# Order of loads, spills and operand making around the borders of the MLP's chunks, and the end of a chunk's MLP block by block

## The chip, the cores and the metric

The kernel runs on one core of a Trainium2 chip. The metric is device time in microseconds of one execution. TensorE (PE) does the matmuls; VectorE (DVE), ScalarE (ACT) and GpSimd (POOL) do everything elementwise; SyncE (SP) issues all DMA transfers of this kernel.

## What is computed

One layer of an encoder on two groups of tokens, 512 and 1024, which the kernel treats as three chunks of 512. The parts that matter here, from the reference:

```python
h = h + jnp.concatenate([o_attn, o_pool], axis=-1) @ w_out
m = _rmsnorm(h, norm_mlp_g)
h = h + jnp.square(jax.nn.relu(m @ w_up)) @ w_down
gate = jax.nn.sigmoid((_rmsnorm(h, norm_ple_g) @ w_ple_gate))
h = h + gate * (p_i @ w_ple_proj)
```

The model width is 1024, the MLP's inner width 4096, all numbers are float32. `_rmsnorm` divides each token by the root of its mean square.

## The kernel before

**Stages.** Input projection (to about 200 us), attention (to about 597), MLP (597 to 1685), gate and final norm (to the end). A float32 product is made from three matmuls: each operand is split in a high part (a cast on ACT) and a low part (a subtraction on DVE or POOL). All SBUF working tiles come from one pool of 49 slots of one size (`slot`); a tile is free when its last reader is done. Activations lie transposed, `hT[c][a]` being block a (of four) of chunk c, 128 x 1024.

**Attention's end.** A loop over `at` issues one group of scores per step, with the softmax and the weighing of earlier groups beside it, and takes pieces from `fill`, a list of other PE work. After it, `while fill` works off the eleven last pieces `po`, the output projection's last ones (twelve matmuls each); two chore steps follow each piece.

**MLP.** Three chunks c, each of 16 pairs g (`Pair`; a pair is two blocks of the inner width). A pair's up projection is seven products of 12 matmuls 128x256 in a scheme after Strassen, in the order 1, 6, 2, 5, 7, 3, 4 (`ORDER`), PSUM tiles px, py, pz, pq. Product i needs an operand tile pair `mo` (i of the chunk, made once) and a weight `w` (made for every pair from the raw weight `wur` by ACT and POOL in `feed`). Four `down` blocks (PSUM pd) of the previous pair go between the products, and each is added to `hT` by DVE (the line of h<-pd). 132 matmuls make a pair. Pairs are counted through, 0 to 47: chunk 1 begins with pair 16, chunk 2 with pair 32.

The MLP's input is never normalised. `h` itself is multiplied by w = the mean square plus epsilon, token by token (`raise_h`, one of four blocks after each product of pair 0), the squares of the up projection of plain h are added to it, and at the end of the chunk h is multiplied by the inverse of w (`invert`, `lower_h`). The DVE executes in the order written, so what stands behind a raise waits for w.

**Making the operands** (`make_m(c)`) is a generator of a chunk before its MLP: h is spilled to DRAM (`spill`, to `h_d`), two tiles m of it loaded per half b, squared on ACT (`sqm`, line 607) and summed; gains and differences are made; seven tiles `mm` per half are split high and low, and stored to `mo_d`; then the sum is split (`sh`), `wait(2)` passes two steps, and the w matmul with ones and one DVE step give w, stored to `w_d`. For chunk 0 each `mo` is loaded again right behind its stores (`load_mo(0, i)`); for the later chunks the loads follow the products of the previous chunk's last pair. `load_ms` brings w back at pair 0, behind the four `load_h`.

**End of a chunk.** During pair 1 of the next chunk `lower_h`, `stat_g` (squares of h summed on DVE, line 590, then the inverse root, spread over the partitions by matmuls), `store_h` (h to `hl_d`) and, for chunk 0, `put_in` (the gate's input split high on ACT, line 1114, low on DVE, line 1115, and stored to `hg_d`) are appended to `chores`.

**What sets the order.** PE, ACT, DVE and POOL execute in the order in which the program is written. Generators in the deque `chores` are advanced by `step()`, one step per product of the MLP (two per piece of the po tail), and only the front one moves. A `yield` therefore is a place where a product's work comes in between; `wait(n)` is n of them. SP's queue alone is ordered by the scheduler: it holds loads and stores, is worked through in order, and an entry waits until its tile is free or its data are there, with all behind it.

## Time and profile before

| | us |
|---|---|
| median of 3 runs (1873.69 to 1878.16) | 1873.84 |
| the profiled execution | 1874.47 |
| its span | 1872.7 |
| mean granted clock of TensorE | 0.983 |

The span is the time on the engines; 1.8 us of the execution lie around it. The profile's views that follow: the page's table of busy time by engine; waits (engine, tile and line that waited, and the engine or transfer whose work ended the wait); windows (the busy time of each engine between two times, with the granted clock as PEclk, and the share of DMA time); and rows of the timeline (start, duration, engine, line, operation, tile written <- tiles read, and in brackets the idle time before it and what ended it).

### The profile page before, as it was taken

How to read it: one execution, taken by the hardware profiler on the slowest of the kernel's cores; microseconds unless marked ns; L12 is line 12 of the kernel's file. 1: busy time of each engine (PE TensorE's matmuls, PEld its weight loads, DVE VectorE, ACT ScalarE, POOL GpSimd, SP SyncE). 2: the span in 40 equal slices, each digit the busy share in tenths (PEclk: the TensorE clock that was granted, in tenths of full speed). 3: DMA queues.
4: the chain of work that ended last, by engine and by line, in shares of the span. 5: the costliest groups of instructions: out<-in, count | busy, mean ns of one | idle time of the engine just before them, and what ended most of it. 6: DMA issues, size and time to landing. Idle time of an engine off the chain costs nothing.

```text
span 1872.7 us, 28563 instructions
## 1 busy us (share of the span) xinstructions
PE 1779.1 (95%) x10540; PEld 1551.8 (83%) x10540; DVE 1248.2 (67%) x1831; ACT 940.8 (50%) x1854; POOL 1030.5 (55%) x909
## 2 busy tenths in 40 slices
PE   9999899999969798999999998999999999999997
PEld 7888777988758687898888887898888898988887
DVE  5667856889864776665569676655686655566555
ACT  6344456678852555444545464445454445443332
POOL 3474864447642685755556475756566556652221
PEclk9999999999989899999999999999999999999998
DMA  6333553012373443532374533523642323362102
GB/s 240 113 136 130 186 208 134 29 68 102 142 247 117 159 147 136 180 113 91 109 284 145 188 133 138 197 90 124 270 164 91 112 91 103 100 242 79 57 10 82
DMA packets 83883, 256.84 MB, mean 137 GB/s; under 512 B 9888, under 2 KB 16416, under 8 KB 83744
## 3 DMA queue, kind: packets, MB, share of 16 engines
q1 hardware_dynamic: 83744, 255.02, 38.6%
q8 instruction: 83, 1.36, 0.3%
q14 instruction: 56, 0.46, 0.1%
HBM read 195.74 MB, written 59.24 MB: 136 GB/s over the span
## 4 chain that ended last, share of the span: by engine, by line
PE 47%; DVE 5%; ACT 3%; POOL 3%; issue 2%; DMA 2%; POOLq 0%; DVEq 0%; SPq 0%; ACTq 0%
PE pd L49 21%; PE pg L49 6%; PE px L49 5%; PE pz L49 5%; PE pq L49 5%; PE py L49 3%; PE pj L49 1%; POOL mm L634 1%; POOL w L784 1%; DVE h L834 1%; DVE r L883 1%; ACT w L783 1%; DMA w<-w_d 1%; DVE wd L814 1%; POOL wd L814 0%
## 5 line engine op out<-in xcount | busy, mean ns | idle before, releaser
L49 PE MATMUL pd<-r,wd 128*128 128x512 f32 x2304 | 576.7, 399 | 12.8 <-DVE r L883 12.2
L49 PEld LDWEIGHTS pd<-r,wd 128*128 128x128 f32 x2304 | 424.5, 190 | 105.4 <-DVE r L883 18.3
L784 POOL TENSOR_TENSOR w<-ws,w 128x512 fp32r<-128x512 f32 x192 | 272.8, 1424 | 242.7 <-ACT w L783 236.6
L784 POOL TENSOR_TENSOR w<-wur,w 128x512 fp32r<-128x512 f32 x144 | 211.4, 1479 | 167.0 <-ACT w L783 157.8
L834 DVE TENSOR_TENSOR h<-pd,h 128x1024 f32<-128x1024 f32 x192 | 233.8, 1218 | 91.7 <-PE pd L49 91.7
L783 ACT CAST w<-ws 128x512 fp32r<-128x512 f32 x192 | 118.5, 617 | 253.4 <-DVE ws L792 224.1
L461 POOL TENSOR_SCALAR pr<-pr,rr 128x512 f32<-128x512 f32 x160 | 111.1, 705 | 143.9 <-DVE rr L456 63.3
L814 DVE TENSOR_TENSOR wd<-wdr,wd 128x512 fp32r<-128x512 f32 x96 | 105.6, 1100 | 109.0 <-ACT wd L813 89.9
L49 PE MATMUL z<-w,x 128*128 128x512 f32 (+1 forms) x864 | 174.8, 358 | 1.9 <-ACT w L159 1.4
L49 PEld LDWEIGHTS pz<-mo,w 128*128 128x128 f32 x1152 | 151.7, 191 | 28.4 <-issue 20.3
L49 PE MATMUL pz<-mo,w 128*128 128x256 f32 x1152 | 154.9, 284 | 18.9 <-issue 14.2
L49 PEld LDWEIGHTS z<-w,x 128*128 128x128 f32 x864 | 142.6, 188 | 28.4 <-ACT w L159 3.3
L49 PE MATMUL pq<-mo,w 128*128 128x256 f32 x1152 | 156.8, 286 | 8.4 <-DVE c L867 4.8
L49 PEld LDWEIGHTS pq<-mo,w 128*128 128x128 f32 x1152 | 147.3, 194 | 9.6 <-issue 9.2
L49 PE MATMUL px<-mo,w 128*128 128x256 f32 x1152 | 153.1, 282 | 0.0
L49 PEld LDWEIGHTS px<-mo,w 128*128 128x128 f32 x1152 | 147.4, 190 | 4.0
L49 PE MATMUL pg<-hg,wg 128*128 128x512 f32 (+1 forms) x768 | 141.1, 338 | 0.2
L814 POOL TENSOR_TENSOR wd<-wdr,wd 128x512 fp32r<-128x512 f32 x96 | 129.1, 1345 | 10.8 <-ACT wd L813 10.8
L472 ACT CAST pt<-tp 128x512 fp32r<-128x512 f32 x160 | 88.3, 591 | 91.3 <-PE tp L53 84.0
L49 PEld LDWEIGHTS pg<-hg,wg 128*128 128x128 f32 x768 | 118.8, 188 | 17.8 <-DVE hg L1115 1.0
L473 DVE TENSOR_TENSOR pt<-tp,pt 128x512 fp32r<-128x512 f32 x160 | 104.2, 684 | 36.3 <-ACT pt L472 35.3
L813 ACT CAST wd<-wdr 128x512 fp32r<-128x512 f32 x192 | 118.8, 619 | 13.5 <-DMA wdr<-in_w_down_dram 11.5
(191 smaller groups left out, 2965.6 us busy)
## 6 DMA issues: line engine op xcount, KB each, us to landing
wur<-in_w_up_dram SPq DMA_DIRECT2D x96, 512.0 KB, 4.1
wdr<-in_w_down_dram SPq DMA_DIRECT2D x96, 512.0 KB, 4.3
mo_d<-mm SPq DMA_DIRECT2D x84, 256.0 KB, 2.6
mo<-mo_d SPq DMA_DIRECT2D x42, 512.0 KB, 6.3
h_d<-h SPq DMA_DIRECT2D x16, 512.0 KB, 2.9
h<-h_d SPq DMA_DIRECT2D x16, 512.0 KB, 8.4
xn<-in_xn_dram SPq DMA_DIRECT2D x12, 512.0 KB, 6.1
qs_d<-qs SPq DMA_DIRECT2D x12, 512.0 KB, 3.0
```

The lines of the kernel that those rows point to most:

```text
L49: last_pe[0] = nc.tensor.matmul(*a, **k).ins
L461: gp.tensor_scalar(p, p, rr, 1.0, op0=ALU.mult, op1=ALU.mult)
L472: sc.copy(self.pt[kt][:, 0], tp)
L473: ve.tensor_tensor(self.pt[kt][:, 1], tp, as32(self.pt[kt][:, 0]), op=ALU.subtract)
L634: el.tensor_tensor(out[:, 1], x, as32(out[:, 0]), op=ALU.subtract)
L783: sc.copy(t[:, 0], x)
L784: gp.tensor_tensor(t[:, 1], x, as32(t[:, 0]), op=ALU.subtract)
L813: sc.copy(hi, self.dr[i][:, h])
L814: (gp, ve)[i].tensor_tensor(lo, self.dr[i][:, h], as32(hi), op=ALU.subtract)
L834: ve.tensor_tensor(h, pd.rearrange("p (a b) -> p a b", a=2), h, op=ALU.add)
L883: ve.tensor_tensor(self.r[i][:, 1], x, as32(self.r[i][:, 0]), op=ALU.subtract)
```

## The change

`make_m` waits five steps, not one, behind the loads of m, and seven, not two, ahead of the w matmul. `load_mo(0, i)` leaves `make_m`: three are issued in the attention loop at steps 99 to 101, and four in the po tail. The first raw weights are loaded at step 96 instead of 94. The first pair's down weights and chunk 0's h are loaded ahead of the po tail and no longer at pair 0. `spill(2)` waits eight steps. For the chunks 0 and 1 `lower_h`, `stat_g`, `store_h` and `put_in` become one generator, `finishing`: a block is lowered on DVE; a step later stored and squared on ACT, and for chunk 0 the gate input's high part is made on ACT; a step later the square is added on POOL (128x1024, three of these and one of 128x512 a chunk, where DVE did it) and the gate input's low part is made on DVE and both are stored. Six steps pass after the sums, then the inverse root follows as before. The loads of h and w at the borders to chunk 1 and 2 stay where they are.

```diff
--- before.py
+++ after.py
@@ -612,7 +612,7 @@
             m = [slot([P, 2, CH], F32, f"m{c}_{2 * i + b}") for i in range(2)]
             for i in range(2):
                 load(m[i], h_d[c][2 * i + b])
-            yield
+            yield from wait(5)
             yield from lagged(squares_of(b, m))
             for i in range(2):
                 for h in range(2):
@@ -634,14 +634,12 @@
                         el.tensor_tensor(out[:, 1], x, as32(out[:, 0]), op=ALU.subtract)
                         for j in range(2):
                             sy.dma_start(mo_d[c][i][j][:, 2 * b:2 * b + 2], as32(out[:, j]))
-                        if c == 0 and b:
-                            load_mo(0, i)
                     yield (lambda x=x, out=out: sc.copy(out[:, 0], x)), low_part
             yield from lagged(pairs())
         sh = slot([P, 2, CH], F32R, f"sh{c}")
         sc.copy(sh[:, 0], acc[:, 0])
         el.tensor_tensor(sh[:, 1], acc[:, 0], as32(sh[:, 0]), op=ALU.subtract)
-        yield from wait(2)
+        yield from wait(7)
         bc = tp_ps(f"w{c}")
         for i in range(2):
             pe.matmul(bc, ones_sb, sh[:, i], start=i == 0, stop=i == 1)
@@ -679,7 +677,10 @@
         out = []
         yield from squares(c, "g", out, e)
         yield from wait((3, 2, 3)[c])
-        bc = yield from rsqrt_rows([out.pop()[:, 0]], CH, f"g{c}")
+        yield from spread_g(c, out.pop())
+
+    def spread_g(c, acc):
+        bc = yield from rsqrt_rows([acc[:, 0]], CH, f"g{c}")
         if c != 1:
             bcs["t"] = slot([P, 2, CH], F32, f"bcs{c}")
         sc.copy(bcs["t"][:, c % 2], bc)
@@ -701,6 +702,7 @@
     away = set()
 
     def spill(c):
+        yield from wait(8 if c == 2 else 0)
         for a in range(4):
             sy.dma_start(h_d[c][a], hT[c][a])
         away.add(c)
@@ -1001,8 +1003,10 @@
         if at == 82:
             for a in range(4):
                 load_h(2, a, h_d[2][a])
-        if at == 94:
+        if at == 96:
             pairs[0].load_up()
+        if at > 98 and at < 102:
+            load_mo(0, ORDER[at - 99])
         for un_ in done:
             un_.finish()
         joining = done
@@ -1060,9 +1064,14 @@
             act()
             yield
 
+    pairs[0].load_down()
+    for a in range(4):
+        load_h(0, a, h_d[0][a])
     while fill:
         fill.popleft()()
         step(2)
+        if len(fill) % 2 and len(fill) < 8:
+            load_mo(0, ORDER[6 - len(fill) // 2])
         if len(fill) % 2 == 0 and len(fill) < 8:
             next(feeding)
     ps_free()
@@ -1106,28 +1115,43 @@
         sc.copy(pp[0], raw)
         e.tensor_tensor(pp[1], raw, as32(pp[0]), op=ALU.subtract)
 
-    def gate_in(c, a):
-
-        hl = [slot([P, 2, CH], F32R, f"hg{c}{a}_{i}") for i in range(2)]
+    def gate_in(c, a, high=None):
+
+        if high is not False:
+            gin[c, a] = [slot([P, 2, CH], F32R, f"hg{c}{a}_{i}") for i in range(2)]
+        hl = gin[c, a]
         for h in range(2):
             g = gple_sb[:, 2 * a + h:2 * a + h + 1]
-            sc.activation(hl[0][:, h], hT[c][a][:, h], AF.Copy, scale=g)
-            ve.scalar_tensor_tensor(hl[1][:, h], hT[c][a][:, h], g, as32(hl[0][:, h]), op0=ALU.mult, op1=ALU.subtract)
-        gin[c, a] = hl
-
-    def store_h(c):
+            if high is not False:
+                sc.activation(hl[0][:, h], hT[c][a][:, h], AF.Copy, scale=g)
+            if not high:
+                ve.scalar_tensor_tensor(hl[1][:, h], hT[c][a][:, h], g, as32(hl[0][:, h]), op0=ALU.mult, op1=ALU.subtract)
+
+    hl_d = [[dram.tile([P, 2, CH], F32, name=f"hl_d{c}_{a}") for a in range(4)] for c in range(2)]
+    def finishing(c):
+
+
+        acc = slot([P, 2, CH], F32, f"sqg{c}")
         for a in range(4):
-            sy.dma_start(hl_d[c][a], hT[c][a])
-        yield
-
-    hl_d = [[dram.tile([P, 2, CH], F32, name=f"hl_d{c}_{a}") for a in range(4)] for c in range(2)]
-    def put_in(c):
-        for a in range(4):
-            gate_in(c, a)
-            for i in range(2):
-                sy.dma_start(hg_d[a][i], flat(gin[c, a][i]))
-            del gin[c, a]
-            yield
+            h = hT[c][a]
+            ve.tensor_tensor(h, h, ws[c].unsqueeze(1).to_broadcast([P, 2, CH]), op=ALU.mult)
+            yield
+            sy.dma_start(hl_d[c][a], h)
+            sq = slot([P, 2, CH], F32, f"sqg{c}{a}") if a else acc
+            sc.activation(sq, h, AF.Square)
+            if c == 0:
+                gate_in(0, a, True)
+            yield
+            if a:
+                gp.tensor_tensor(acc, acc, sq, op=ALU.add)
+            if c == 0:
+                gate_in(0, a, False)
+                for i in range(2):
+                    sy.dma_start(hg_d[a][i], flat(gin[c, a][i]))
+            yield
+        gp.tensor_tensor(acc[:, 0], acc[:, 0], acc[:, 1], op=ALU.add)
+        yield from wait(6)
+        yield from spread_g(c, acc)
 
     hg_d = [[dram.tile([P, D], F32, name=f"hg_d{a}{i}") for i in range(2)] for a in range(4)]
 
@@ -1154,21 +1178,18 @@
         c, g = pair.c, pair.g
         raising = None
         if g == 0:
-            for a in range(4):
-                load_h(c, a, h_d[c][a])
+            if c:
+                for a in range(4):
+                    load_h(c, a, h_d[c][a])
             load_ms(c)
             raising = raise_h(c)
         if g == 1:
             chores.append(invert(c))
             if c:
                 load_ms(c - 1)
-                chores.extend((lower_h(c - 1, ve), stat_g(c - 1, ve), store_h(c - 1)))
-            if c == 1:
-                chores.append(put_in(0))
+                chores.append(finishing(c - 1))
             if c < 2:
                 chores.append(make_m(c + 1, ve, gp))
-        if n == 0:
-            pair.load_down()
         splits = pair.split_down()
 
         def between(i):
```

**SP at the end of attention**, where `make_m(0)` makes the operands. `mm` is a tile made by ACT and the low part's engine, `mo_d` its place in DRAM, `mo` the tile loaded from there for the MLP. Before:

```order
L636 DMA mo_d_61_265<-mm_61_5666 128x512
L636 DMA mo_d_20_266<-mm_21_5711 128x512
L56 DMA mo_61_5717<-mo_d_61_265 128x1024
L56 DMA mo_20_5766<-mo_d_20_266 128x1024
L636 DMA mo_d_21_267<-mm_21_5711 128x512
L636 DMA mo_d_50_268<-mm_51_5761 128x512
L56 DMA mo_21_5767<-mo_d_21_267 128x1024
L56 DMA mo_50_5811<-mo_d_50_268 128x1024
L636 DMA mo_d_51_269<-mm_51_5761 128x512
```

and now:

```order
L636 DMA mo_d_10_262<-mm_11_5927 128x512
L636 DMA mo_d_60_264<-mm_61_5964 128x512
L636 DMA mo_d_11_263<-mm_11_5927 128x512
L636 DMA mo_d_20_266<-mm_21_6005 128x512
L636 DMA mo_d_61_265<-mm_61_5964 128x512
L636 DMA mo_d_50_268<-mm_51_6051 128x512
L636 DMA mo_d_21_267<-mm_21_6005 128x512
L56 DMA wur_00_6097<-in_w_up_dram 128x1024
L636 DMA mo_d_51_269<-mm_51_6051 128x512
```

Each load of an `mo` stood two to four entries behind the stores that it reads; now stores follow one another, with loads of raw weights in between.

**SP at the border to the MLP.** h_d<-h are the spills of chunk 2, `wur` raw up weights, h<-h_d and w<-w_d what pair 0 of chunk 0 raises. Before, behind the store of w (three entries ahead of this piece):

```order
L705 DMA h_d_0_312<-h_5543 128x1024
L705 DMA h_d_1_313<-h_5545 128x1024
L705 DMA h_d_2_314<-h_5547 128x1024
L56 DMA wur_10_6523<-in_w_up_dram 128x1024
L705 DMA h_d_3_315<-h_5549 128x1024
L56 DMA wur_11_6524<-in_w_up_dram 128x1024
L56 DMA h_6548<-h_d_0_304 128x1024
L56 DMA h_6550<-h_d_1_305 128x1024
L56 DMA h_6552<-h_d_2_306 128x1024
L56 DMA h_6554<-h_d_3_307 128x1024
L56 DMA w_6556<-w_d_259 128x512
```

and now, from the store of w on (chunk 0's h is already loaded before it, and the spills of chunk 2 come behind it):

```order
L647 DMA w_d_259<-sqm_4189 128x512
L56 DMA mo_50_6400<-mo_d_50_268 128x1024
L56 DMA mo_51_6401<-mo_d_51_269 128x1024
L56 DMA mo_70_6438<-mo_d_70_270 128x1024
L56 DMA mo_71_6439<-mo_d_71_271 128x1024
L56 DMA mo_30_6474<-mo_d_30_272 128x1024
L56 DMA mo_31_6475<-mo_d_31_273 128x1024
L56 DMA mo_40_6509<-mo_d_40_274 128x1024
L56 DMA mo_41_6510<-mo_d_41_275 128x1024
L56 DMA wur_10_6531<-in_w_up_dram 128x1024
L56 DMA wur_11_6532<-in_w_up_dram 128x1024
L56 DMA w_6556<-w_d_259 128x512
```

The w load stood behind four spills and four h loads; now it stands behind eight mo and two wur loads. On PE the w matmul, which before came in the last steps of the attention loop, now stands behind the third of the eleven po pieces.

**DVE at the end of chunk 0.** `hg` is the gate's input, `c` and `r` belong to the current pair's squares, and the rows h<-pd add its down blocks. Before, in pair 20:

```order
L834 TENSOR_TENSOR h_10033<-pd_22_10852,h_10033 128x1024
L871 TENSOR_TENSOR c_3_10697<-pz_3_10807,u_3_10696 128x256
L877 TENSOR_TENSOR c_3_10697<-pq_3_10829,u_3_10696 128x256
L798 TENSOR_TENSOR ws_41_10822<-wur_40_10676,wur_41_10677 128x512
L1115 SCALAR_TENSOR_TENSOR hg_1_10914<-h_6548,gple_sb,hg_0_10913 128x512 x2
L883 TENSOR_TENSOR r_30_10698<-c_3_10697,r_30_10698 128x512
L883 TENSOR_TENSOR r_31_10699<-c_3_10697,r_31_10699 128x512
L834 TENSOR_TENSOR h_10035<-pd_23_10923,h_10035 128x1024
L801 TENSOR_TENSOR ws_41_10822<-wur_40_10676,ws_40_10821 128x512
L1115 SCALAR_TENSOR_TENSOR hg_1_10966<-h_6550,gple_sb,hg_0_10965 128x512 x2
```

and now, in pair 17:

```order
L1137 TENSOR_TENSOR h_6341<-h_6341,w_10253 128x1024
L836 TENSOR_TENSOR h_10033<-pd_02_10399,h_10033 128x1024
L873 TENSOR_TENSOR c_1_10256<-pz_1_10355,u_1_10255 128x256
L879 TENSOR_TENSOR c_1_10256<-pq_1_10378,u_1_10255 128x256
L800 TENSOR_TENSOR ws_21_10370<-wur_20_10233,wur_21_10234 128x512
L1128 SCALAR_TENSOR_TENSOR hg_1_10435<-h_6341,gple_sb,hg_0_10434 128x512 x2
L885 TENSOR_TENSOR r_10_10257<-c_1_10256,r_10_10257 128x512
L885 TENSOR_TENSOR r_11_10258<-c_1_10256,r_11_10258 128x512
L836 TENSOR_TENSOR h_10035<-pd_03_10468,h_10035 128x1024
L803 TENSOR_TENSOR ws_21_10370<-wur_20_10233,ws_20_10369 128x512
L1137 TENSOR_TENSOR h_6343<-h_6343,w_10253 128x1024
```

The low part of hg followed its high part on ACT within one step, and the sums and lowers lay in other pairs; now a block is lowered (h<-h,w), and its low part is made two steps later.

## The prediction

> **What bounds the kernel now.** I read the page's busy table first.
>
> ```profile
> span 1872.7 us, 28563 instructions
> PE 1779.1 (95%) x10540; PEld 1551.8 (83%) x10540; DVE 1248.2 (67%) x1831; ACT 940.8 (50%) x1854; POOL 1030.5 (55%) x909
> ```
>
> PE is busy for 95%, so at most 93.6 us of idle PE can go, beside time in which PE works at a lower clock. The change keeps the matmuls, so I next asked what PE waits for, and what the others wait for in the same places.
>
> ```profile
> PE pz L49 <- issue: 14.2, 3, 13.1
> PE pd L49 <- DVE r L883: 12.2, 11, 3.7
> PE S L49 <- ACT pr L449: 10.3, 2, 6.7
> PE w L49 <- POOL sh L643: 6.8, 2, 3.7
> PE pq L49 <- DVE c L867: 4.8, 1, 4.8
> PE pz L49 <- DVE u L863: 4.7, 1, 4.7
> ...
> ACT sqm L607 <- DMA m<-h_d: 16.9, 4, 9.0
> ACT pr L449 <- DMA mo_d<-mm: 10.5, 2, 6.6
> DVE h L663 <- DMA w<-w_d: 24.8, 3, 10.9
> ```
>
> The columns are total, count and longest. A few single waits hold most of it, and each has a neighbour below it that waits for a DMA. I then cut the span at the first matmul of successive pairs (and of score groups before the MLP) and took the busy table of the stretches that hold these waits.
>
> ```profile
> core 0: us, PE busy (x) PEld busy (x) DVE busy (x) ACT busy (x) POOL busy (x), PEclk, DMA share, GB/s
> 469.22:476.38 7.16, 4.38 (x30) 3.78 (x29) 3.04 (x8) 3.71 (x9) 0.01 (x1) 1.00 0.60 213
> 476.38:480.52 4.14, 4.14 (x30) 3.75 (x29) 4.11 (x8) 3.68 (x10) 3.73 (x5) 1.00 0.32 129
> 495.70:504.55 8.85, 8.85 (x50) 6.71 (x49) 8.69 (x16) 8.15 (x21) 7.70 (x9) 1.00 0.87 317
> 524.21:556.95 32.74, 19.09 (x86) 14.07 (x84) 15.38 (x28) 14.86 (x36) 12.85 (x16) 0.84 0.74 249
> 597.26:647.88 50.62, 35.06 (x218) 32.17 (x217) 30.55 (x38) 18.65 (x36) 24.70 (x18) 0.83 0.54 196
> 690.22:718.06 27.84, 23.05 (x133) 20.41 (x132) 16.37 (x20) 13.01 (x25) 17.93 (x14) 0.94 0.60 218
> 760.68:787.67 26.99, 23.33 (x135) 20.45 (x134) 16.38 (x20) 12.46 (x24) 17.85 (x13) 0.94 0.51 184
> 956.47:980.05 23.58, 21.86 (x133) 19.05 (x132) 15.82 (x20) 7.82 (x16) 10.99 (x9) 1.00 0.57 212
> 956.47:1047.17 90.70, 87.45 (x540) 77.24 (x538) 70.79 (x86) 44.67 (x81) 53.48 (x40) 1.00 0.44 151
> 1047.17:1101.83 54.66, 47.30 (x265) 41.34 (x264) 40.58 (x50) 29.51 (x56) 25.80 (x19) 0.91 0.44 169
> 1122.98:1151.72 28.74, 24.02 (x134) 21.34 (x132) 16.35 (x22) 13.27 (x26) 16.28 (x13) 0.88 0.55 194
> 1173.34:1201.14 27.80, 23.87 (x135) 20.58 (x134) 18.56 (x19) 15.02 (x29) 26.18 (x19) 0.94 0.68 233
> 1328.05:1419.57 91.52, 87.53 (x540) 77.07 (x539) 71.86 (x87) 44.79 (x81) 54.14 (x40) 1.00 0.45 157
> 1440.67:1651.87 211.20, 211.20 (x1321) 189.98 (x1320) 124.77 (x170) 101.25 (x190) 125.00 (x91) 1.00 0.30 99
> 604.00:614.00 10.00, 0.52 (x5) 0.32 (x3) 1.56 (x2) 2.70 (x6) 2.01 (x2) 0.79 1.02 408
> ```
>
> The last row but one is ten undisturbed pairs: 21.12 us each, PE without a gap, clock 1.00. Against it the other pairs show their excess. The sum below is made against the profiled execution, 1874.47 us with its launch; the median shown is 0.63 us less.
>
> **The change part by part.**
>
> *A, squares of chunk 0's first half (469.22).* The step takes 7.16 where the next one takes 4.14. The squares on ACT stand one step behind the loads they read, and PE waits at the end of the chain for a DVE tile. With five steps the load is there. Gain 3.0, at least 0 if the longer hold of the m tiles makes another engine wait. The same holds at the second m loads of chunks 1 and 2 (terms D and H).
>
> *B, five score steps (524.21 to 556.95).* Three normal steps take 8.85, so five take 14.75, and the w matmul half a microsecond: 15.3, hence 17.5 too much. SP issues in order; each operand load waits until its own stores have landed (2.6 us in the row below) and holds the following stores, whose tiles therefore stay taken; ACT waits for a free tile (the 10.5 above) and PE for ACT (the 10.3). Without the loads the stores stream. Gain 16.6, 0.9 kept for normal waits; from 0 (the tiles stay scarce for another reason) to 17.5.
>
> ```profile
> w_d<-sqm SPq DMA_DIRECT2D x3, 256.0 KB, 2.5
> mo_d<-mm SPq DMA_DIRECT2D x84, 256.0 KB, 2.6
> ...
> 581.72 15.70 PE L49 MATMUL po<-cat,wo 128*128 128x256 f32 x132
> 601.51 1.58 PE L49 MATMUL pz<-mo,w 128*128 128x256 f32 x12
> 602.93 1.59 PE L49 MATMUL pq<-mo,w 128*128 128x256 f32 x12
> 617.67 2.90 PE L49 MATMUL pz<-mo,w 128*128 128x256 f32 x12 [13.15 <-issue]
> ...
> 610.03 1.22 DVE L663 TENSOR_TENSOR h<-h,w 128x1024 f32<-128x1024 f32 x1 [10.95 <-DMA w<-w_d]
> 611.17 0.42 DVE L855 TENSOR_TENSOR u<-py,u 128x256 f32<-128x256 f32 x1
> 614.29 0.74 DVE L814 TENSOR_TENSOR wd<-wdr,wd 128x512 fp32r<-128x512 f32 x1 [2.70 <-ACT wd L813]
> ```
>
> *C, pair 0 and 1.* Groups of 12 start 1.42 apart, so seven products need 9.9; pairs 0 and 1 together (597.26 to 647.88) took 50.62 instead of 9.9 + 21.1: 19.6 lost. w lands at 610.03 because it is queued behind the spills of chunk 2 and four h loads; DVE waits in order on the raise, and PE on DVE. In the changed order the h loads are ahead of the tail and the spills behind w. Ahead of w now stand eight mo loads and two wur loads. The w matmul sits behind the third of eleven po pieces (15.70/11 = 1.43 each): 581.7 + 4.3 + about 1.3 for the DVE step = 587.3. To move from there: w out and in (2 x 0.26 MB) and ten blocks of 0.524 MB, 5.77 MB; at the 408 GB/s of the window 604 to 614 14.1 us, and 1.9 latency (2.5 less 0.6 of transfer). w lands near 603.3, 6.0 behind the first MLP matmul instead of 12.8. Then raise 1.22, u 0.42, wd 0.74, raise 1.2, u 0.4 let the second pz start near 607.3 instead of 604.3: a gap of 2.9, about 1.6 and 1.9 at the next two waits as now, 1.5 of slow clock, so 8 lost. Gain 11.7. Bounds: w in time, 19.6; a block every 2.6 us, the pace of the stores, puts w near 616 and that pz near 620 instead of 617.67, a loss of 3. I stay with 11.7, for the 10-us window that moves loads and nothing else is the nearest row.
>
> Moved with it: the four spills of chunk 2 leave eight steps later, four tiles stay taken that much longer, and the tiles for wd, h and mo of pair 0 are taken earlier. In the queue after the change no load of chunk 0 stands behind a store that needs these tiles, so I price this at nothing; the cover is the po tail of 15.70, and without it the first down load would come late, which the 19.6 already bounds from the other side. The two later borders keep their loads where they are, so their 2.5 each (below) stays (the raise waits 24.8 in three).
>
> *D, E, H, I (690, 760, 1122, 1173).* Excess over 21.12: 6.7, 5.9, 7.6, 6.7. D and H are the m loads again (pq waits 4.8, pz 4.7), E and I the w matmul, which waits for sh from POOL (6.8 in all). A step is a product, 21.12/7 = 3.0 us; five or seven steps are 15 to 21 us, and the waits were under 9.0. The wait is a yield of the generator and no instruction, so nothing queues behind it on ACT or POOL; on SP the w store moves with it, and its reader comes only at the next border, ten pairs on. Leaving 0.3 each: gain 25.7; least 0, if POOL is what is late and the delay only moves it.
>
> *G, end of chunk 0 (956.47 to 1101.83).* 90.70 and 54.66 against 84.48 and 42.24: 18.6 too much, of which 23.58 − 21.12 = 2.5 in pair 16 (956.47 to 980.05) is the border's own w load, not touched. In pairs 20 and 21 the low part on DVE stands right behind ACT's high part and then r, then pd:
>
> ```profile
> 1049.02 1.91 DVE L1115 SCALAR_TENSOR_TENSOR hg<-h,gple_sb,hg 128x512 fp32r<-128x512 f32 x2 [3.40 <-ACT hg L1114]
> ...
> 1080.68 4.38 PE L49 MATMUL pd<-r,wd 128*128 128x512 f32 x11 [2.96 <-DVE r L883]
> ```
>
> The new order puts a step between them, and brings forward by a pair or more the eight stores to hg_d and four to hl_d that go with it; they spread over twelve steps where before four hl stores left in one, beside a DMA share of 0.44, so I price them at nothing: the weight loads between them are made at least a pair ahead of their use, and a store takes 2.6. Without that lead they are a rival below. What is left should look like chunk 1's end (1328.05), which has no gate input: 91.52 less 84.48 less the same 2.5 = 4.5. Gain 18.6 − 2.5 − 4.5 = 11.6. *J, end of chunk 1:* its four lowers come three steps apart; gain 1.3 of the 4.5.
>
> *Adds to POOL.* No row has POOL add 128x1024. Nearest:
>
> ```profile
> L784 POOL TENSOR_TENSOR w<-wur,w 128x512 fp32r<-128x512 f32 x144 | 211.4, 1479 | 167.0 <-ACT w L783 157.8
> 699.34 1.76 DVE L814 TENSOR_TENSOR wd<-wdr,wd 128x512 fp32r<-128x512 f32 x1 [2.54 <-POOL mm L634]
> ```
>
> Twice the elements: between 1.48 and 2.96; I take 2.6. Eight in all, 21 us, over ten pairs in which POOL idles 8.6 us each (125.00 of 211.20): hidden; without that cover up to 24 us. The wd split that took 0.74 alone takes 1.76 beside POOL work, so each add can cost DVE about two such microseconds: 16 in all, where DVE idles 8.6 per pair. I put 2 us for it on the path. The Trainium skill's "GPSIMD Engine Reference", 1. Specifications, speaks against this part: the two engines share their SBUF interfaces, and a VectorE instruction with two SBUF inputs contends. The two wd rows agree; by that rule alone the adds would cost up to those 16 us and the time would be 1820.
>
> Of the clock: after the 2.96 gap eleven matmuls take 4.38, where a full down block takes (21.12 − 9.9)/4 = 2.8. So each gap near 3 us costs some 1.5 more, and these go with the gaps. The Trainium skill's "TensorE: Matmul & The Clock Gate", Part 1, lets the clock halve only after an idle window of about 3.4 us; by that rule the gap left at the border would cost nothing more, and the time be 1.5 less. The trace shows it at 2.96.
>
> Sum: 3.0 + 16.6 + 11.7 + 25.7 + 11.6 + 1.3 − 2 = 67.9; 1874.5 − 67.9 = 1806.6, against the median 1806.
>
> **The rivals.**
> - *The border stays.* The mo and wur blocks now ahead of w arrive at the pace of 2.6 us. For it: window 524 moved 249 GB/s only. Against: the 408. C gives −3 instead of 11.7: 1821.
> - *The waits are only postponed.* POOL's high share in these pairs (17.85 of 26.99, 26.18 of 27.80) makes sh late however long one waits, and the adds crowd it. Against: POOL idles 8.6 us of an undisturbed pair. D, E, H, I give 6 instead of 25.7: 1826. With the first: 1841.
> - *Tiles stay scarce in B*, because the mo loads still come at step 99 and take seven pairs of tiles: 1823.
> - *The stores hold the weight loads.* SP's queue at the end of chunk 0 now alternates stores, whose data come one step after the other, with wur and wdr loads, as it did with the mo loads in B. Then G gains nothing: 1818. Against: the loads have a pair's lead there, and had none in B.
> - *The adds slow DVE on the path.* The 16 us of its sharing with POOL fall where DVE is what PE waits for: 1820. Against: DVE's 8.6 us of idle time in a pair.
> - *More is gained*: the border gap and chunk 1's remainder vanish: 1806 − 8 − 2 = 1796.
> - *Slower*: with PE busy throughout, the granted clock falls below 1.00 everywhere. 68 of gain are eaten once 1779 us run at 0.963; at 0.95 it is 1874 + 94 − 68 = 1900. Against it stand 211 us without a gap at 1.00.
> - *It does not do what it says*: the scheduler issues the loads as late as before at every place: within a few microseconds of 1874. Against: the order of the SP queue shown ahead.
>
> **How the numbers follow.** Forecast 0.49 (its own bounds 1799 to 1814); border 0.14; postponed 0.11; both 0.03; tiles 0.04; stores 0.05; adds 0.03; more 0.05; slower 0.03; nothing 0.03. From "more" to "postponed" with the bounds of C and G on top: 1796 to 1838, which leaves out some 0.09 of the named cases and the error of my sums. About 0.3% is what a measurement here can tell. Faster 0.94, same 0.03, slower 0.03.
>
> **What would show it.** Right: pairs at 21.1 to 21.6 where D, E, H, I were; no wait S <- pr over 1 us; raise waiting about 4 to 6 us for w; the first MLP pair near 16 us. Wrong: w landing more than 10 us behind the first MLP matmul; w <- sh waits over 2 us; a granted clock under 1.00 in pairs without gaps; DVE, not PE, without idle time at the chunks' ends.

## The result and the profile after

| | before | after |
|---|---|---|
| median | 1875.63 us (4 runs, 1873.69 to 1878.16) | 1828.65 us (4 runs, 1827.95 to 1830.56) |
| ratio | | 0.975, 95% interval 0.9733 to 0.9767 |
| span of the profiled execution | 1872.7 us | 1826.2 us |

The change is faster by 47.0 us in the medians, 46.5 in the spans. The forecast was 1806, with 1796 to 1838 as its range: the time lies in the range, and a third of the forecast gain (46.5 of 67.9) is missing.

The page of the changed kernel, span and busy times by engine:

```profile
span 1826.2 us, 28559 instructions
PE 1769.2 (97%) x10540; PEld 1543.7 (85%) x10540; DVE 1247.3 (68%) x1823; ACT 939.5 (51%) x1854; POOL 1047.5 (57%) x917
```

PE's busy time fell by 9.9 us for the same matmuls: that part of the gain is clock, the other 36.6 of the 46.5 are waits. What PE still waits for (engine, tile and line that waited, what ended the wait; total, count, longest; "issue" stands where the profile shows nothing that PE waited for):

```profile
PE pd L49 <- DVE r L885: 11.8, 13, 2.0
PE pz L49 <- issue: 8.9, 3, 7.8
...
PE pz L49 <- DVE u L865: 2.1, 1, 2.1
...
PE pq L49 <- DVE c L869: 0.8, 1, 0.8
PE S L49 <- ACT pr L449: 0.7, 2, 0.4
```

S <- pr fell from 10.3 to 0.7, pq <- c from 4.8 to 0.8, and w <- sh (6.8) and po <- ob (2.8) are gone. What stays is pd <- r, 11.8 after 12.2, and one wait of 7.8 in pair 0. The windows of the same places, from first px to first px (start:end, length, busy times, granted clock, DMA share, GB/s):

```profile
470.36:474.52 4.16, 4.16 (x30) 3.75 (x29) 3.90 (x9) 3.64 (x9) 2.28 (x4) 1.00 0.71 276
580.11:623.74 43.63, 34.65 (x218) 31.62 (x217) 26.51 (x38) 19.00 (x36) 22.79 (x18) 0.88 0.67 259
665.89:687.07 21.18, 21.18 (x133) 19.07 (x132) 15.15 (x16) 11.94 (x24) 19.59 (x15) 1.00 0.58 198
730.43:751.57 21.14, 21.14 (x133) 19.00 (x132) 15.04 (x17) 13.13 (x27) 19.83 (x15) 1.00 0.50 179
...
921.40:1020.47 99.07, 90.02 (x529) 78.21 (x528) 77.83 (x88) 48.08 (x87) 60.71 (x41) 0.97 0.52 185
1020.47:1063.93 43.46, 43.46 (x275) 39.19 (x274) 28.53 (x38) 22.38 (x44) 27.32 (x22) 1.00 0.33 111
1085.05:1106.13 21.08, 21.08 (x133) 19.03 (x132) 14.88 (x17) 11.94 (x23) 18.66 (x14) 1.00 0.56 198
...
1128.79:1149.83 21.04, 21.04 (x134) 18.93 (x132) 19.81 (x25) 13.95 (x27) 13.29 (x10) 1.00 0.25 84
1277.16:1371.63 94.47, 87.98 (x529) 77.11 (x528) 68.96 (x80) 44.14 (x81) 60.26 (x41) 0.98 0.44 153
1394.08:1605.06 210.98, 210.98 (x1321) 189.91 (x1320) 124.71 (x170) 101.27 (x191) 125.05 (x91) 1.00 0.31 99
```

Pairs 4, 7, 23 and 25, which took 26.99 to 28.74, take 21.04 to 21.18 with no idle PE. The end of chunk 0 falls from 90.70 + 54.66 to 99.07 + 43.46: 8.4 more in its first four pairs, 11.2 less in the next two. The end of chunk 1 is longer, 94.47 against 91.52. By stretch, the profiled executions against one another:

| stretch | forecast gain | before | after | gain |
|---|---|---|---|---|
| up to the MLP's first matmul (A, B) | 19.6 | 597.26 | 580.11 | 17.1 |
| pairs 0 and 1 (C) | 11.7 | 50.62 | 43.63 | 7.0 |
| pairs 2 to 15 (D, E) | 12.0 | 308.58 | 297.66 | 10.9 |
| pairs 16 to 21 (G) | 11.6 | 145.36 | 142.54 | 2.8 |
| pairs 22 to 31 (H, I) | 13.7 | 226.22 | 213.22 | 13.0 |
| pairs 32 to 36 (J) | 1.3 | 112.62 | 116.92 | −4.3 |
| the rest | 0 | 432.02 | 432.09 | −0.1 |

Forecast in all 69.9, less 2 for adds beside DVE. G and J miss 14.4 between them, C 4.7, A and B 2.5.

In pairs 18 and 19 of the changed kernel DVE's rows show where the time is (start, duration):

```profile
980.43 4.58 DVE L1128 SCALAR_TENSOR_TENSOR hg<-h,gple_sb,hg 128x512 fp32r<-128x512 f32 x2
...
992.09 1.42 DVE L1128 SCALAR_TENSOR_TENSOR hg<-h,gple_sb,hg 128x512 fp32r<-128x512 f32 x2 [0.88 <-ACT hg L1126]
...
994.35 1.22 DVE L1137 TENSOR_TENSOR h<-h,w 128x1024 f32<-128x1024 f32 x1
995.49 4.55 DVE L885 TENSOR_TENSOR r<-c,r 128x512 fp32r<-128x512 f32 x2
```

and POOL's:

```profile
979.91 2.85 POOL L1146 TENSOR_TENSOR sqg<-sqg,sqg 128x1024 f32<-128x1024 f32 x1
982.72 1.74 POOL L786 TENSOR_TENSOR w<-wur,w 128x512 fp32r<-128x512 f32 x1
...
996.67 2.82 POOL L1146 TENSOR_TENSOR sqg<-sqg,sqg 128x1024 f32<-128x1024 f32 x1
999.45 3.46 POOL L786 TENSOR_TENSOR w<-ws,w 128x512 fp32r<-128x512 f32 x2
```

Two gate inputs take 1.42 with POOL idle and 4.58 beside POOL's add and what follows it: the one wholly beside the add takes 2.88, the other, beside the 128x512 instruction behind it, 1.78. The two r take 4.55: 1.77 and, beside the add, 2.86, where one alone takes 0.68. On PE, u (which stands behind the gate input) and r end these waits:

```profile
986.63 2.69 PE L49 MATMUL pz<-mo,w 128*128 128x256 f32 x12 [2.12 <-DVE u L865]
...
997.31 0.96 PE L49 MATMUL pd<-r,wd 128*128 128x512 f32 x3 [1.48 <-DVE r L885]
```

At the border to the MLP the queue of transfers is full. SP, PE and DVE there, and a window:

```profile
569.83 0.32 SPq L647 DMA_DIRECT2D w_d<-sqm  x1
570.24 8.06 SPq L56 DMA_DIRECT2D mo<-mo_d  x8
579.21 1.56 SPq L56 DMA_DIRECT2D wur<-in_w_up_dram  x2
581.77 0.33 SPq L56 DMA_DIRECT2D w<-w_d  x1
...
591.48 1.23 DVE L661 TENSOR_TENSOR h<-h,w 128x1024 f32<-128x1024 f32 x1 [9.54 <-DMA h_d<-h]
...
595.21 2.90 PE L49 MATMUL pz<-mo,w 128*128 128x256 f32 x12 [7.82 <-issue]
```

```profile
560.00:600.00 40.00, 32.19 (x247) 31.49 (x246) 19.20 (x35) 9.99 (x20) 14.18 (x12) 0.89 1.01 396
```

The DMA share is 1.01 over 40 us. The raise starts at 591.48, 11.4 behind the first MLP matmul at 580.11, where the forecast had w 6.0 behind it (before: 12.8). The row names a spill as what ended the wait; the transfer that landed just ahead of the raise, at 591.38 in the trace, is w. Its load stands in SP's queue behind the others and left only at 581.77.

### The profile page after: what moved, and what is told of

Its sections match the earlier page's. It is cut to its first block, busy times and chain, and to the rows that moved or that the text cites. A ratio compares the mean times of both kernels' runs of the same rounds, so it can differ in the third digit from the quotient of the medians.

```text
span 1826.2 us, 28559 instructions
## 1 busy us (share of the span) xinstructions
PE 1769.2 (97%) x10540; PEld 1543.7 (85%) x10540; DVE 1247.3 (68%) x1823; ACT 939.5 (51%) x1854; POOL 1047.5 (57%) x917
## 5 line engine op out<-in xcount | busy, mean ns | idle before, releaser
L49 PE MATMUL pd<-r,wd 128*128 128x512 f32 x2304 | 572.2, 396 | 13.1 <-DVE r L885 11.8
L885 DVE TENSOR_TENSOR r<-c,r 128x512 fp32r<-128x512 f32 x96 | 75.2, 788 | 72.6 <-ACT c L882 45.0
```

Source lines behind the costliest of these rows:

```text
L49: last_pe[0] = nc.tensor.matmul(*a, **k).ins
L885: ve.tensor_tensor(self.r[i][:, 1], x, as32(self.r[i][:, 0]), op=ALU.subtract)
```

## The experiments

Each kernel was timed beside the kernel before on the same chip; medians, and ratio with 95% interval to that before. In the table after them the stretches of all their profiled executions stand side by side.

**The waits alone**, in the kernel before:

```diff
-            yield
+            yield from wait(5)
...
-        yield from wait(2)
+        yield from wait(7)
```

> The kernel before with the two longer waits alone (five steps behind the m loads, seven ahead of the w matmul). Theory: A, D, E, H and I are the waits' doing: 3.0 + 10.9 + 13.0 = 27 us off 1875.6, and up to 3 more where the m loads stood in pair 21: 1846 to 1849. Rival (the waits only postpone, the gain there came from other parts): 1860 or more.

Measured 1844.76 us, ratio 0.9837 (0.9822 to 0.9852): 1.2 us under the theory's 1846 to 1849. But by stretch it is not quite the theory: pairs 2 to 15 gain 10.6, as in the changed kernel, the stretch up to the MLP 7.6, pairs 16 to 21 3.9, and pairs 22 to 31 only 5.3 of the 13.0. There pair 24 now takes 26.62, where the changed kernel has 22.66. So in chunk 0's MLP (pairs 2 to 15) the waits are enough; in chunk 1's (pairs 22 to 31) the stall of pair 23 is gone (21.43), and another stands one pair later.

Pair 21 falls from 25.92 to 21.17 by the waits alone. The row of 1080.68 in the prediction, eleven slow matmuls behind a gap of 2.96, lies in this pair of the kernel before, and what stood on DVE ahead of its r was not the gate input but a square of the operand making, which waited for the loads of m:

```profile
1078.70 1.33 DVE L609 TENSOR_TENSOR sqm<-sqm,sqm 128x512 f32<-128x512 f32 x1 [4.34 <-ACT sqm L607]
1079.95 1.28 DVE L883 TENSOR_TENSOR r<-c,r 128x512 fp32r<-128x512 f32 x2
```

**The old end of a chunk**, all else as changed (`finishing(c - 1)` replaced by `lower_h`, `stat_g`, `store_h` and, for chunk 0, `put_in`):

```diff
-                chores.append(finishing(c - 1))
+                chores.extend((lower_h(c - 1, ve), stat_g(c - 1, ve), store_h(c - 1)))
+            if c == 1:
+                chores.append(put_in(0))
```

> The changed kernel with the chunk's end as before (lowering, squares, stores and gate input one after the other), all else as changed. Theory 1: the new end gave 2.8 us at the end of chunk 0 and took 4.3 at the end of chunk 1, so the old one is worth about 1.5 us less time, 1826 to 1829, with wait(5) alone removing part of the old excess of pairs 20 and 21 (12.4): if the 2.96 gap there came from the m loads and not from the gate input, 1820 to 1824. Rival (the new end gains the forecast 12.9): 1840.

Measured 1827.50 us, ratio 0.9747 (0.973 to 0.9763): the new end of a chunk is worth nothing in sum that can be told here. By stretch it moves time: with the old end pairs 16 to 21 take 4.6 us less, pairs 32 to 36 4.3 less, pairs 22 to 31 8.9 more. In pair 20 the old wait of DVE for ACT's high part is there again (3.45; pair 27.51). Pair 24 has the stall of the kernel with the waits alone (27.66); DVE's row names it:

```profile
1105.60 1.45 DVE L800 TENSOR_TENSOR ws<-wur,wur 128x512 f32<-128x512 f32 x1 [4.76 <-DMA mo_d<-mm]
```

A tile for the weights' sums is not free until a store of operands has landed. With the new end this wait is not there. That it frees tiles earlier is my reading; no run took only that away. A rival stays open: with another number of steps ahead of it, the operand making falls at other places of the pairs. The second loads of m leave 7.1 us into pair 24 in the changed kernel, and at its start with the old end.

**The adds on DVE**, block by block as in the change:

```diff
-                gp.tensor_tensor(acc, acc, sq, op=ALU.add)
+                ve.tensor_tensor(acc, acc, sq, op=ALU.add)
...
-        gp.tensor_tensor(acc[:, 0], acc[:, 0], acc[:, 1], op=ALU.add)
+        ve.tensor_tensor(acc[:, 0], acc[:, 0], acc[:, 1], op=ALU.add)
```

> The changed kernel (1828.65 us) with one difference: the sums of squares in the chunk's end are added on DVE again instead of POOL, block by block as in the change. Theory 1 (POOL's 128x1024 adds slow DVE's two-operand instructions in pairs 18, 19 and 35, where DVE rows of 0.70 take 2.3): those pairs fall from 21.1 + 5.4, 5.3 and 3.9 to about 21.1 + 1.5 each, 10 us less in all, 1818 to 1820. Rival (the block-by-block order itself crowds DVE): DVE gets eight adds of 1.2 us more, the pairs stay or grow, 1828 to 1835.

Measured 1826.53 us, ratio 0.9738 (0.9723 to 0.9754). Pairs 18, 19 and 35 take 25.15, 26.84 and 25.20, after 26.52, 26.46 and 24.98: theory 1 in this form fails, and no pair grew by what DVE took over either. The adds now stand on DVE itself, ahead of what PE waits for; in pair 18, just ahead of a gate input and then u:

```profile
978.62 2.31 DVE L1146 TENSOR_TENSOR sqg<-sqg,sqg 128x1024 f32<-128x1024 f32 x1
```

**No full adds** (the sums then lack the squares of blocks 1 to 3):

```diff
-            if a:
-                gp.tensor_tensor(acc, acc, sq, op=ALU.add)
```

> The changed kernel without the six full adds of squares on POOL at the chunks' ends (the sums of squares of blocks 1 to 3 are left out). Theory 1 (what is left of it): if sharing between these adds and DVE is the cost, pairs 18, 19 and 35 fall from 26.5, 26.5 and 25.0 to 22 to 23, 10 us less, 1819. Theory 3 (place of the lowering and of the gate input on DVE): they stay above 24.5, 1825 to 1828.

Measured 1816.93 us, ratio 0.9689 (0.9672 to 0.9706), 11.7 less than the changed kernel. Pairs 18, 19 and 35: 23.90, 23.27, 21.10. Together with the run before it: the six adds cost about 11 us in these places (9.7 of it in the three pairs), whichever engine makes them. The rows show two ways: on POOL they lengthen what DVE does meanwhile, on DVE they take its time ahead of u and r. That these two ways are the whole of it is not shown. The gate inputs and r in the same pairs:

```profile
980.17 2.44 DVE L1128 SCALAR_TENSOR_TENSOR hg<-h,gple_sb,hg 128x512 fp32r<-128x512 f32 x2
...
993.06 2.36 DVE L885 TENSOR_TENSOR r<-c,r 128x512 fp32r<-128x512 f32 x2
```

2.44 and 2.36 in place of 4.58 and 4.55.

**r ahead of the last step:**

```diff
-            after(4)
             for i, x in enumerate((c1, c2)):
                 ve.tensor_tensor(self.r[i][:, 1], x, as32(self.r[i][:, 0]), op=ALU.subtract)
+            after(4)
```

> The changed kernel with the two low parts of r issued on DVE ahead of the last product's step of chores and feeding, not behind it. Theory 3 (in pairs 18, 19 and 35 a lowered block or a gate input stands on DVE just ahead of r, on which the next pair's first down block waits): the waits of pd for r (1.5, 1.8 and 2.1 us, with the slow clock behind them) go, pairs 19 and 35 fall to about 22.5, pair 18 keeps its wait for u, 6 to 7 us off 1828.65: 1821 to 1823. Rival (DVE has too much to do there in all): the wait moves to u, c or the weights, 1827 to 1831; if the weights' sums come late in every pair, slower.

Measured 1844.59 us, ratio 0.9839 (0.9819 to 0.9858): 16 us slower than the changed kernel. pd <- r stays, and the next product's tiles wait in its place:

```profile
PE pd L49 <- DVE r L884: 12.9, 13, 1.9
PE pz L49 <- issue: 8.8, 3, 7.8
PE pq L49 <- DVE c L869: 6.8, 4, 2.1
PE pz L49 <- DVE u L865: 3.5, 2, 3.1
```

```profile
974.23 0.69 DVE L884 TENSOR_TENSOR r<-c,r 128x512 fp32r<-128x512 f32 x1 [3.78 <-ACT c L882]
```

r waits for ACT's squares (the row is of pair 18; in the changed kernel that wait is 0.44); what now stands behind it on DVE, and ran in that wait, comes later (pair 18 takes 31.10, pair 4 23.93). Moving r is no cure; theory 3 gave the wrong time.

**The adds later**, behind all four blocks, one per step, and on DVE:

```diff
-            if a:
-                gp.tensor_tensor(acc, acc, sq, op=ALU.add)
...
+        for sq in sqs[1:]:
+            ve.tensor_tensor(acc, acc, sq, op=ALU.add)
+            yield
         gp.tensor_tensor(acc[:, 0], acc[:, 0], acc[:, 1], op=ALU.add)
-        yield from wait(6)
+        yield from wait(3)
```

> The changed kernel with the three full adds of squares of each chunk's end moved behind its four blocks, on DVE, one per step, and three steps fewer waited behind them. Theory 1b (the adds cost 11 us because they fall among a block's lowering and gate input, on whichever of the two engines; one by one in steps without these they are hidden): pairs 18 and 35 fall to 24 and 21 to 22, pair 19 to 23 to 24, 8 to 10 us less than the changed kernel: 1819 to 1821. Rival (each add costs its time on the path wherever it is): 1826 to 1829.

Measured 1824.63 us, ratio 0.9723 (0.9709 to 0.9738). Pairs 18, 19 and 35 fall to 23.93, 24.72 and 21.88, near what they are without the adds, but pairs 20 and 36 rise from 22.4 to 24.4 and 24.3. Some 4 of the adds' 11 us are gone, half of the expected 8 to 10, and not all of that is shown to be the place: this kernel differs from the changed one in the engine too, and against the adds on DVE block by block it is 1.9 us faster, with intervals that overlap.

**w loaded behind its store:**

```diff
         sy.dma_start(w_d[c], acc[:, 1])
+        if c == 0:
+            load_ms(0)
...
-            load_ms(c)
+            if c:
+                load_ms(c)
```

> The changed kernel with chunk 0's w loaded directly behind its store, ahead of the last eight operand loads, instead of at pair 0. Theory 2 (w is late at the first border because 21 MB/50 us of loads queue ahead of it at a full DMA rate of 408 GB/s: it landed 11.3 us behind the first MLP matmul): w lands at or before that matmul, the gap of 7.8 us and the slow clock behind it go, pairs 0 and 1 fall from 43.6 to 33 to 36: 1818 to 1821. Rival (the volume is the bound: what w gains the operand loads lose): the gap stays and moves to the products 5 to 4 or to pair 1, 1826 to 1832.

Measured 1825.97 us, ratio 0.9736 (0.9719 to 0.9753), 2.7 under the changed kernel, with intervals that overlap. In the profiled execution, the longest of the four, the border did not gain: pairs 0 and 1 take 45.05 against 43.63. The raise now has its w, and DVE waits a few entries on for the raw weights of pair 1:

```profile
581.60 1.22 DVE L663 TENSOR_TENSOR h<-h,w 128x1024 f32<-128x1024 f32 x1
...
595.83 1.18 DVE L794 TENSOR_TENSOR ws<-wur 128x512 f32<-128x512 f32 x1 [6.29 <-DMA wur<-in_w_up_dram]
```

SP's rows and a window show what else this edit did:

```profile
572.11 0.32 SPq L709 DMA_DIRECT2D h_d<-h  x1
578.13 0.32 SPq L56 DMA_DIRECT2D w<-w_d  x1
578.50 5.60 SPq L56 DMA_DIRECT2D mo<-mo_d  x8
```

```profile
576.00:580.00 4.00, 4.00 (x37) 4.00 (x36) 1.13 (x3) 1.18 (x3) 3.79 (x3) 1.00 0.43 158
```

SP's queue stood until the store of w had landed, the last eight operand loads left from 578.50 on and not from 570.24, and the DMA share is 0.43 for 4 us in a stretch where every block is waited for. The wait moved on, as the rival said. But that the volume of loads alone is the bound is not shown, since this kernel also holds the queue.

**Shorter waits for chunk 0:**

```diff
-            yield from wait(5)
+            yield from wait(5 if c else 3)
...
-        yield from wait(7)
+        yield from wait(7 if c else 3)
```

> The changed kernel with shorter waits for chunk 0 alone: three steps behind the m loads and three ahead of the w matmul (five and seven in the later chunks as changed). Theory 2 (the operand loads of chunk 0 start too late, at 559, so that 40 us at the full 408 GB/s end only at 600 and w lands 11.3 us behind the first MLP matmul): eight steps less, the loads start some 7 us earlier and w lands 7 us earlier, the gap of 7.8 falls to 1 to 2, pairs 0 and 1 to 36 to 38: 1821 to 1824. Rival (tiles are not free earlier, so the loads cannot start earlier): no change, 1827 to 1830.

Measured 1823.66 us, ratio 0.9723 (0.9708 to 0.9738). The store of w leaves at 554.55 and not at 569.83, ahead of the operand loads; the load of w, behind them, leaves 4 us earlier than in the changed kernel (577.75, not 581.77), and so much earlier the raise finds its w:

```profile
554.55 0.33 SPq L647 DMA_DIRECT2D w_d<-sqm  x1
...
587.32 1.33 DVE L661 TENSOR_TENSOR h<-h,w 128x1024 f32<-128x1024 f32 x1 [5.61 <-DMA w<-w_d]
```

Pair 0 takes 17.92 in place of 20.46. The shift is 4 us, of the expected 7, and pairs 0 and 1 take 41.59, not 36 to 38: the expected time was met, but only 2.0 of the 5.0 us come from the border, and the intervals of the two kernels just overlap.

**Both:**

> As the kernel with shorter waits for chunk 0, and w loaded directly behind its store, ahead of all operand loads. Theory 2: the store now leaves before the queue is full, so w's way out and in costs about 4 us and not 11, and neither the operands nor the raw weights lose by it what w gains: pairs 0 and 1 at 33 to 36, 1818 to 1821. Rival (the volume ends at the same time, and DVE then waits for the next pair's raw weights as it did with w loaded early alone): 1823 to 1827.

Measured 1823.91 us, ratio 0.9723 (0.9707 to 0.974). Pairs 0 and 1 take 40.18, 3.5 less than in the changed kernel, but above the expected 33 to 36; what is left there is two waits of 2.5 on PE, which end just behind u and c, instructions of DVE that follow a raise. For the raw weights of pair 1 DVE now waits 0.28. In time it cannot be told from the last: once the store leaves before the queue is full, w's place in the queue is worth little.

**The operand loads inside the making**, as before the change (the two `load_mo` outside taken out):

```diff
+                        if c == 0 and b:
+                            load_mo(0, i)
...
-        if at > 98 and at < 102:
-            load_mo(0, ORDER[at - 99])
...
-        if len(fill) % 2 and len(fill) < 8:
-            load_mo(0, ORDER[6 - len(fill) // 2])
```

> The changed kernel with chunk 0's operand loads issued again inside the operand making, each right behind its stores. Theory 4 (such a load holds SP's queue until its stores have landed, and with it the tiles that ACT waits for): the score steps before the MLP lose again what they lost in the kernel with the longer waits alone, whose MLP began at 589.6 against 580.1, so it begins at 588 to 591; what the border gains back, because fewer operand loads stand ahead of w, is up to 7: 1831 to 1838. Rival (the longer waits and the earlier h loads made that gain): the MLP begins at 580 to 583 and the time is 1822 to 1830.

Measured 1833.66 us, ratio 0.9778 (0.9761 to 0.9794), 5.0 above the changed kernel. The MLP begins at 584.89 and pairs 0 and 1 take 47.37: 4.8 and 3.7 worse; the gap in pair 0 is 11.7. The time is in the theory's range, but the MLP begins between the two forecasts, and the border lost where the theory had it gain. The window from the last group of scores to the MLP, of the waits alone, of this kernel and of the changed one:

```profile
541.69:589.63 47.94, 41.22 (x274) 36.33 (x275) 22.20 (x44) 17.30 (x36) 18.54 (x19) 0.93 0.78 262
```

```profile
541.87:584.89 43.02, 38.00 (x275) 33.76 (x276) 22.97 (x44) 17.23 (x36) 17.86 (x19) 1.00 0.79 269
```

```profile
541.97:580.11 38.14, 36.84 (x274) 33.84 (x275) 22.93 (x44) 17.01 (x36) 18.57 (x19) 1.00 0.87 314
```

All three reach the last group of scores at 541.7 to 542.0, where the kernel before came to it at 560.0: the longer waits alone cure the five slow score steps, because they carry the end of the operand making into the po tail. There it costs 9.8 us, of which the place of the loads is 4.9. The other 4.9 belong to the rest of the change ahead of the MLP, by my reading the earlier loads of h and down weights and the later spills; no run parts them.

**Late adds with both changes for chunk 0:**

> The kernel with late adds, with the shorter waits for chunk 0 and w loaded right behind its store as well. Both theories: the gains are in different stretches and add, 5 us at the border and 8 to 10 at the chunks' ends: 1814 to 1816. If the adds are not hidden: 1821 to 1824.

Measured 1819.41 us, ratio 0.970 (0.9685 to 0.9714). Faster than both kernels: the border's 3.5 and the late adds' gain add, without reaching the 1814 to 1816.

**The half add a step earlier**, in that kernel:

```diff
             ve.tensor_tensor(acc, acc, sq, op=ALU.add)
-            yield
+            if sq is not sqs[-1]:
+                yield
         gp.tensor_tensor(acc[:, 0], acc[:, 0], acc[:, 1], op=ALU.add)
-        yield from wait(3)
+        yield from wait(4)
```

> The last kernel (late adds, chunk 0's shorter waits, w behind its store; 1819.4 us) with POOL's half add of the sums one step earlier, in the step of the third add. Theory 3, what is left of it (POOL's half add now runs beside r on DVE, 1.26 for its second half where 0.69 is usual, and pd waits 1.46 for it in pairs 20 and 36): these pairs fall from 24.4 to 22.5, 4 us less, 1815 to 1817. Rival (the half add only moves on to another instruction that PE waits for): 1818 to 1821.

Measured 1819.12 us, ratio 0.969 (0.9673 to 0.9707), not to be told from the last. Pairs 20 and 36 fall by 0.8 and 0.6, not 1.9; r runs at 0.69 again, but the waits behind it are still 0.9.

Stretches in us:

| | to the MLP | 0, 1 | 2 to 15 | 16 to 21 | 22 to 31 | 32 to 36 |
|---|---|---|---|---|---|---|
| before | 597.26 | 50.62 | 308.58 | 145.36 | 226.22 | 112.62 |
| after | 580.11 | 43.63 | 297.66 | 142.54 | 213.22 | 116.92 |
| waits alone | 589.63 | 50.30 | 297.94 | 141.51 | 220.90 | 112.71 |
| old end | 579.91 | 43.75 | 297.67 | 137.93 | 222.10 | 112.64 |
| adds on DVE | 579.93 | 43.17 | 297.65 | 140.41 | 212.97 | 116.72 |
| no full adds | 579.84 | 44.88 | 297.65 | 135.71 | 213.08 | 111.82 |
| r first | 578.97 | 43.64 | 301.80 | 147.79 | 219.56 | 118.44 |
| late adds | 582.16 | 43.61 | 297.66 | 140.25 | 213.27 | 114.50 |
| early w | 579.86 | 45.05 | 297.75 | 143.66 | 213.20 | 117.09 |
| shorter for chunk 0 | 579.89 | 41.59 | 297.22 | 143.83 | 213.00 | 115.14 |
| both for chunk 0 | 580.42 | 40.18 | 297.73 | 143.58 | 213.32 | 116.63 |
| loads inside | 584.89 | 47.37 | 297.20 | 140.94 | 213.23 | 116.58 |
| late adds, both | 579.65 | 40.18 | 297.86 | 140.00 | 214.12 | 113.92 |
| half add earlier | 580.32 | 40.20 | 298.94 | 140.67 | 213.43 | 113.24 |

The five kernels that leave the changed end of a chunk alone (after, early w, the two for chunk 0, loads inside) spread over 2.9 us in the column 16 to 21 and 2.0 in 32 to 36, so differences there are good to about that. Six kernels share the code up to the MLP (after, old end, adds on DVE, no full adds, r first, late adds): they begin it within 3.2 us of one another, and those that also share pairs 0 and 1 (all but r first) spread over 1.7 there.

## Why the prediction was right or wrong, point by point

The time lies in the range, but outside the bounds 1799 to 1814 of the forecast itself. It lies near the 1826 of the rival "the waits are only postponed"; that is chance, as D, E, H and I, which that rival puts at 6, gained 23.9. Of the signs of being right two came (pairs 4, 7, 23 and 25 at 21.04 to 21.18, S <- pr at most 0.4) and two did not (the raise waited 9.5 for w, the first pair took 20.46); of the signs of being wrong one came, w more than 10 us behind the first MLP matmul.

- *A* held: the step takes 4.16.
- *B*: the place held (17.1 for A and B against 19.6), the mechanism only in part. That it matters where the operand loads stand is shown, and with the border it is worth 5 us in time. The score steps themselves were cured by the longer waits, which I had credited with nothing there. The rival "tiles stay scarce in B" is not seen: S <- pr fell from 10.3 to 0.7.
- *C*: the pace held, the start did not. Between the w store's issue and the raise I counted what is queued behind the store (5.77 MB at 408 GB/s, 14.1 us) and took 1.9 us of latency for it to land. But the same change puts the operands, the down weights and h ahead of the store; it was issued at 569.83 with six such loads (two of down weights, four of h) still out, and in the trace landed only at 577.92. Those 6.2 us are the term that was left out: w 11.3 behind the first matmul, not 6.0. Six blocks of 0.524 MB at that rate are 7.7 us, near the 8.1 that the store took. The runs with an earlier start move the wait in this sense; the run with w ahead of its queue moves it to the raw weights. The rival "the border stays" (a loss of 3) is not borne out either: the border gained 7.0.
- *D, E* held (10.9 for 12.0, with no idle PE left in pairs 4 and 7). *H, I* held in size (13.0 for 13.7), but the reason given was the waits alone, and these give 5.3; the rest needs the new end of the chunk, without which DVE waits for a tile in pair 24; why it does is open. The rival "the waits are only postponed" was right there for the kernel with the waits alone, though through a tile and not through POOL.
- *G, J* failed, and here the step that failed is "hidden", of the adds: 2.0 us on the path, because DVE idles 8.6 us in a pair. They cost 11 us (without them 1816.93), as an idle share of the pair is no cover for a DVE instruction that lengthens just ahead of u or r. The rival that names this, "the adds slow DVE on the path", had 0.03 and a price of 14 more than forecast; measured with the full adds out, it is 11.7. Without them G gains 9.7 of its 11.6 and J 0.8 of its 1.3, so the adds are most of the 14.4 missed. The size taken for one add, 2.6, was near: 2.82 to 2.87 at the end of chunk 0, 2.36 to 2.40 at the end of chunk 1. That the new end would separate high and low part of the gate input was right (pair 20 fell from 28.74 to 22.41; with the old end it is 27.51). But G also read pair 21's excess of 4.8 as the gate input's, and it was the m loads': the waits alone take it away.
- *The clock*: 0.983 to 0.991, and PE's busy time 9.9 us less; with no idle time the granted clock stayed at 1.00 (1394 to 1605), so the rival on the slow side has nothing for it. A gap of 2.12 (986.63) was followed by a group of 2.69 in place of 1.58: the trace again has slow matmuls behind gaps shorter than the 3.4 us of the Trainium skill's "TensorE: Matmul & The Clock Gate", Part 1. The windows on both sides (PE busy for 1.29 of 3.41 us, then a clock of 0.51):

```profile
983.53:986.94 3.41, 1.29 (x7) 0.79 (x6) 3.41 (x4) 0.00 (x0) 0.93 (x1) 0.99 0.35 132
986.94:990.35 3.41, 3.41 (x17) 3.16 (x16) 3.41 (x6) 0.49 (x1) 0.00 (x0) 0.51 0.79 261
```

- The other rivals: "the stores hold the weight loads" is not seen: PE's waits in pairs 17 to 20 are for r (5.0 in all) and u (2.1) on DVE, none for weights.

## What to carry to other kernels

Price work that is moved to an idle engine by the instructions beside which it will run, and by what stands right behind those, not by the idle share of a stretch: eleven microseconds sat in six adds that both engines had time for. When loads are moved ahead of something urgent, count the bytes still on their way at that moment too, not only those issued after it. At the full DMA rate here an earlier start moved the wait by 4 us, and an earlier place in the queue hardly moved the time. And check a gain stretch by stretch even when the total is right: the waits alone came within 2 us of their forecast total with two stretches off.

## What the runs showed of the hardware

DVE instructions with two SBUF operands did not only run at half speed beside POOL's add: one of 128x512 took 0.68 (r) or 0.74 (hg) alone, 1.77 or 1.78 beside a 128x512 instruction of POOL, and 2.86 or 2.88 wholly beside the 128x1024 add, which itself took 2.82 and 2.85. So in these rows it lasted about as long as the POOL instruction beside it, four times its own time. Instructions with an operand in PSUM kept theirs: h<-pd took 1.21 beside other POOL instructions (974.96, 999.96), and a u<-pz that lay mostly beside an add (1336.01) took 0.41. The Trainium skill's "GPSIMD Engine Reference", 1. Specifications, names the contention; the sizes stand in this trace. And with seven loads of 512 KB still out at a DMA share of 1.01, a transfer took about ten microseconds to land, a small one hardly less: w, 256 KB, was issued at 581.77 and landed at 591.38, 9.6 us, where the loads around it took 9.5 to 10.2.
